# mLSTM's gates made in steps beside two scans, and 64x64 merge blocks whose directions take turns

## The chip, the cores and the metric

The kernel runs on one core of one Trainium2 chip. The number of a run is the device time of one execution, in microseconds. Three runs of the kernel before gave 1412.16, 1409.82 and 1408.49 us, so its time is a median of 1409.82 us.

A core has engines with a queue each, and each queue is worked off in order: PE (matrix products), DVE (elementwise work, scans along a row), ACT (functions and scaled copies), POOL (elementwise work), and SP, which here only issues DMA transfers. An instruction that waits for another engine or for a transfer holds up everything that is queued behind it on its own engine.

## The reference, cut to what matters

One layer: a norm, one projection into two mixers (gated DeltaNet, GDN, with 8 heads, and mLSTM with 4), each run over the tokens in both directions, then a merge, an output projection and a gated MLP. There are 256 context tokens and 512 latent tokens. What the change touches are mLSTM's gates and the triangular solve of GDN:

```
ig = soft_cap(ml_i + ml_igate_b)                 # soft_cap(x) = 15 * tanh(x / 15)
lf = log_sigmoid(soft_cap(ml_f + ml_fgate_b))
m_t = max(lf_t + m_{t-1}, ig_t)                  # the stabiliser, by direction and head
bc = cumsum(lf) in each chunk
dmat = bc[:, None] - bc[None, :] + ig[None, :]   # then exp(dmat - m_t): mLSTM's weights
...
# GDN, by head and direction:
a_strict = (k * beta) @ k^T * decay
sol = triangular_solve(a_strict, rhs, lower, unit_diagonal)
```

mLSTM's gates are needed when its first head is prepared and scanned, after all of GDN's scans but the last few. GDN's solve is done by an explicit inverse of blocks of 128 tokens, built from 16x16 inverses (POOL) by merges of 16, 32 and 64 (PE).

## The kernel before, in words

Weights are streamed from memory, split on ACT and POOL or DVE into a high and a low part (L102, L103), and multiplied in three passes (`mm3`, L113 and L114). Head h of GDN is prepared by `gdn_prep(h)`: projections k, q, v, z (`acc`, in two PSUM banks that take turns, so that a projection starts when the one before the last has been read out by `conv_silu`, L595 to L599, or by L724 and L726), the decay rows `Eg` (loaded by DMA from `gd`, the GDN gates' own transposed rows, L631; finished on DVE by L646 and on ACT by L647; two buffers), the products of k with itself (`pkk`, L701 and L704), the 16x16 inverses (`inverses`: DVE cuts the diagonal blocks out, L765 to L767, a DMA `scr` and one back, a chain on POOL, L778 and L780, DMAs `scx` and `cdx`, and back into SBUF on ACT by L805), the products of q and k (L709, L713).

`merges(h)` then makes the inverse of a 128 block: `y0p` and `w0p` from 16 to 32 rows (L812, L819), `y1p` and `wp` from 32 to 64 (L844, L852), `y2p` and `w2p` from 64 to 128 (L865, L873). Each product is a matmul on a part of the array, named by its row and column strips. Each of the two directions has its own order of blocks. `gdn_scan(h)` is the scan over six chunks, `gdn_tail` what follows it.

`gdn_gates` makes GDN's gates from the gates' logits `Z` (128 rows by 768 tokens, in `oTg`, which is free until the first head's result is written at its end). The rows for the decays go through a copy `grr` (L502) and a DMA to `gd` (L504), and the DMAs of `Eg` and `qs` read `gd`.

`ml_gates` (L506 to L586) makes mLSTM's gates from the same logits: a tanh of all of `Z` (L520), a log sigmoid (L524 to L527), two cumulative sums in two directions and the running maximum in two directions (the five scans L531 to L535), the differences from chunk to chunk (L540 to L567), three exponentials (L564, L568, L569), two DMAs out (`r1d`, `ged`), two back in (`ge`), and twelve transposes on PE (L582) with four copies (L583) into `colA` and `colB`.

What sets the order: the program is written as Python generators; `drive` (L1128) takes a scan's steps, and between them the steps of other work (`bulk`, the preparation of a head three further on, and `side`, such as the next head's merges at the steps in `MERGE`). The text's order gives each instruction a priority; a scheduler then lays each engine's queue, and takes an instruction of lower priority ahead where it holds its operands and the engine would be idle by the scheduler's own reckoning. A `follow` adds a tie: this instruction stays behind an anchor on its engine. Before, `ml_gates` is written between the preparation of heads 0 to 2 and the first merges, with a priority that is `LATER` = 400 places down (L1170 to L1173) and with its first instruction tied behind the last `conv_silu` on ACT.

Of the kernel before, what the change touches and what calls it, by code (L numbers as in the profile page):

```python
# [60 lines left out]
LATER = 400  # L61
# [7 lines left out]
class Kern:  # L69
# [355 lines left out]
    def gates_rows(self, psx, psc):  # L425
# [4 lines left out]
        Z = self.grow[0]  # L430
# [75 lines left out]
    def ml_gates(self):  # L506

        nc, cp, hold = self.nc, self.cp, self.hold
        Q = 64
# [16 lines left out]
        nc.scalar.activation(t2, t2, AF.Ln, bias=1.0)
        nc.vector.scalar_tensor_tensor(L, z, 0.0, t2, ALU.min, ALU.subtract)  # L527
# [3 lines left out]
        nc.vector.tensor_tensor_scan(G[F, :], rm[F, :], L[F, :], 0.0, ALU.mult, ALU.add)  # L531
# [43 lines left out]
        for d in range(2):  # L575
            nc.sync.dma_start(self.ge[:, d, 8:12].rearrange("p r c -> p (r c)"),
                              ged[32 * d + 8 : 32 * d + 12, :].rearrange("r c -> (r c)").unsqueeze(0).broadcast_to([P, 4 * NCH]))
        for (T_, col) in ((TA, self.colA), (TB, self.colB)):
            for (c0, c1) in ((0, 4), (4, 6)):
                ps = self.pt([P, 512], "prep", "ps_gt")  # L580
                for c in range(c0, c1):
                    nc.tensor.transpose(ps[:, (c - c0) * P : (c - c0 + 1) * P], T_[:, c * P : c * P + P], self.ident)  # L582
# [203 lines left out]
    def merges(self, h):  # L786
# [750 lines left out]
```

## Time and profile before

| | |
|---|---|
| median of three runs | 1409.82 us (1408.49 to 1412.16) |
| the profiled execution | 1413.52 us, of which the span from first to last instruction is 1411.6 us |
| PE busy | 1326.0 us (94%), mean granted clock 0.966 |
| DVE / ACT / POOL busy | 908.5 us / 588.5 us / 507.8 us |
| head 0's scan begins on PE (L919) | at 187.8 us |
| mLSTM's gates on DVE | from 141.9 to 182.4 us |
| merges of heads 0 to 7 | from 150.4 to 591 us |

A row of the timeline view gives start, length, engine, source line, operation, the tiles written and read, a count, and in brackets how long its engine had been idle before it and what ended that. A row of the windows view gives, for a stretch, its length, the busy time of each engine with the number of its instructions, the granted clock of PE (1.00 is full speed), the share of the DMA engines and GB/s.

### The profile page before, as it was taken

The numbers are of one execution on the slowest core, as the hardware profiler recorded it, in microseconds if no ns is written. First come the engines' busy times: TensorE is split into PE (matmuls) and PEld (weight loads), VectorE is DVE, ScalarE is ACT, GpSimd is POOL, SyncE is SP. The second block draws the span as 40 slices with busy tenths as digits, with TensorE's granted clock in tenths as the row PEclk, the third lists the DMA queues.
The fourth block names the chain that finished last, engine by engine and source line by source line (L and its number), as shares of the span: only waits on it lengthen the run. The fifth ranks groups of instructions, "written<-read, shape, count | busy, mean of one in ns | idle before, by whom it ended". The sixth has DMA issues, their size and how long they took to land. (4 is left out here: it accounts for less than half of the span.)

```text
span 1411.6 us, 24202 instructions
## 1 busy us (share of the span) xinstructions
PE 1326.0 (94%) x9436; PEld 1121.7 (79%) x9436; DVE 908.5 (64%) x1860; ACT 588.5 (42%) x1283; POOL 507.8 (36%) x626
## 2 busy tenths in 40 slices
PE   5888699999999999999899999999989999999997
PEld 4777588878887887889788877788878888888886
DVE  6748973748575774655654464644559879879933
ACT  6555554545555554323233334432234333333331
POOL 4426131130321303243735662000135555555552
PEclk9999799999999999999999999999989999999999
DMA  8633233231322322354524442364323333233321
GB/s 244 152 88 93 56 80 83 74 102 37 89 77 69 82 50 77 106 151 117 144 75 112 114 118 61 98 202 139 126 69 111 90 98 102 84 104 90 104 90 60
DMA packets 233232, 141.85 MB, mean 100 GB/s; under 512 B 32977, under 2 KB 215518, under 8 KB 233118
## 3 DMA queue, kind: packets, MB, share of 16 engines
q1 hardware_dynamic: 233118, 140.31, 35.3%
q8 instruction: 74, 1.21, 0.4%
q14 instruction: 40, 0.33, 0.1%
HBM read 134.47 MB, written 5.82 MB: 99 GB/s over the span
## 5 line engine op out<-in xcount | busy, mean ns | idle before, releaser
L1507 DVE SCALAR_TENSOR_TENSOR y<-pu,fw,y 128x441 f32<-128x441 f32 (+2 forms) x352 | 230.0, 691 | 38.5 <-ACT y L1498 32.9
L137 POOL TENSOR_TENSOR rs<-pw_t,mhalf 128x1 f32<-128x1 f32 x14 | 8.2, 584 | 168.3 <-DVE pw_t L136 168.3
L137 POOL TENSOR_TENSOR kh<-pw_t,phalf 128x6 f32<-128x6 f32 x8 | 11.1, 1390 | 124.1 <-DVE pw_t L136 124.1
L293 POOL TENSOR_TENSOR aw<-aw,sc 128x512 f32<-128x512 f32 x32 | 40.0, 1256 | 31.1 <-DMA aw<-in_w_ada_dram 31.0
L915 DVE SCALAR_TENSOR_TENSOR X<-p,colA,vt 128x128 f32<-128x128 f32 x80 | 24.3, 346 | 33.9 <-PE p L911 33.7
L797 POOL TENSOR_TENSOR qs<-qs,qT 128x512 f32<-128x512 f32 x16 | 20.8, 1304 | 62.2 <-DMA qs<-gd 50.1
L773 POOL MEMSET gx<- 96x16 f32 x8 | 1.0, 123 | 115.4 <-DMA gx<-scr 115.4
L927 ACT ACTIVATE v<-p,sc 128x128 f32<-128x128 f32 x80 | 25.4, 367 | 34.4 <-PE p L919 34.3
L931 PE MATMUL p<-v,kt 128*128 128x128 f32 x160 | 29.8, 302 | 10.5 <-ACT v L927 10.5
L778 POOL TENSOR_TENSOR iv_t<-gx 96x14 f32<-96x14 f32 (+6 forms) x112 | 36.0, 322 | 7.5
L1076 DVE SCALAR_TENSOR_TENSOR C<-C,ge,mpc 128x257 f32<-128x257 f32 x32 | 15.3, 479 | 36.3 <-PE mpc L1072 36.2
L780 POOL TENSOR_TENSOR gx<-gx,iv_t 96x14 f32<-96x14 f32 (+6 forms) x112 | 34.8, 311 | 8.6
L1498 ACT ACTIVATE y<-pu,fw 128x512 f32<-128x512 f32 x44 | 30.0, 683 | 16.1 <-PE pu L114 6.8
L931 PEld LDWEIGHTS p<-v,kt 128*128 128x128 f32 x160 | 23.0, 195 | 16.8 <-ACT v L927 14.9
L646 DVE SCALAR_TENSOR_TENSOR Eg<-Eg,colA,mask 128x128 f32<-128x128 f32 x96 | 33.1, 411 | 3.9 <-DMA Eg<-gd 3.9
L1449 POOL TENSOR_TENSOR al<-y,ah 128x512 fp32r<-128x512 f32 x22 | 28.7, 1304 | 17.3 <-ACT ah L1448 15.8
L1281 DVE SCALAR_TENSOR_TENSOR x<-x,py 128x512 f32<-128x512 f32 x16 | 11.0, 686 | 36.6 <-PE py L114 36.6
L938 DVE SCALAR_TENSOR_TENSOR S<-S,ge,p 128x128 f32<-128x128 f32 x64 | 19.3, 343 | 18.2 <-PE p L931 17.1
L911 PE MATMUL p<-S,kT 128*128 128x128 f32 x160 | 29.9, 289 | 0.0
L944 ACT ACTIVATE v<-p,sc 128x128 f32<-128x128 f32 x64 | 23.1, 378 | 15.8 <-PE p L931 15.0
L1459 DVE TENSOR_TENSOR fd_t<-pd,m 128x512 f32<-128x512 f32 x8 | 5.3, 685 | 37.5 <-PE pd L114 37.5
L598 ACT ACTIVATE cv_t<-cv_y 128x512 f32<-128x512 f32 (+1 forms) x40 | 21.8, 546 | 17.2 <-DVE cv_y L597 14.2
(1235 smaller groups left out, 4699.4 us busy)
## 6 DMA issues: line engine op xcount, KB each, us to landing
aw<-in_w_ada_dram SPq DMA_DIRECT2D x41, 256.0 KB
uw<-in_w_ada_dram SPq DMA_DIRECT2D x16, 512.0 KB
Eg<-gd SPq DMA_DIRECT2D x16, 384.0 KB
gx<-in_w_ada_dram SPq DMA_DIRECT2D x23, 256.0 KB
qs<-gd SPq DMA_DIRECT2D x16, 256.0 KB
xn<-in_x_dram SPq DMA_DIRECT2D x4, 512.0 KB
Em<-r1d SPq DMA_DIRECT2D x8, 256.0 KB
mwo_0r<-in_w_in_dram SPq DMA_DIRECT2D x4, 512.0 KB
```

The source lines that it names most:

```text
L293: eng.tensor_tensor(w, w, self.sc[:, 4 * i : 4 * i + 4, 0:1].broadcast_to([P, 4, P]), ALU.mult)
L646: self.follow(nc.vector.scalar_tensor_tensor(E[:, c, :], E[:, c, :], self.colA[:, c, d, row : row + 1], self.mask[d], ALU.add, ALU.min), "v")
L778: eng.tensor_tensor(t, Bi[:, 0:j, j : j + 1].broadcast_to([8 * NB, j, n]), Bi[:, j : j + 1, j + 1 :].broadcast_to([8 * NB, j, n]), ALU.mult)
L780: g = eng.tensor_tensor(Bi[:, 0:j, j + 1 :], Bi[:, 0:j, j + 1 :], t, ALU.add)
L911: g = nc.tensor.matmul(p1[:, d, :], kT[:, c * P : c * P + P], S[d], start=True, stop=True)
L915: self.anchor["v"] = nc.vector.scalar_tensor_tensor(X[d], p1[:, d, :], self.colA[:, c, 2 + d, h : h + 1], vt[:, c, :], ALU.mult, ALU.subtract)
L927: nc.scalar.activation(v3[d], p2[:, d, :], AF.Copy, scale=sc[d][:, 2 + j, c : c + 1])
L931: g = nc.tensor.matmul(p3[:, d, :], kt[:, c, :], v3[d], start=True, stop=True)
L944: nc.scalar.activation(v2, p2[:, d, :], AF.Copy, scale=sc[d][:, j, c : c + 1])
L1449: nc.gpsimd.tensor_tensor(al[:, j, :], ys[0], ah[:, j, :].bitcast(F32), ALU.subtract)
L1498: nc.scalar.activation(y, ps, AF.Copy, scale=tap(0, 0))
L1507: g = nc.vector.scalar_tensor_tensor(o, u3[:, r0 + dy : r1 + dy, c0 + dx : c1 + dx], tap(dy, dx), o, ALU.mult, ALU.add)
```

## The change

Two things. First, `ml_gates` becomes a generator: its body is cut by `yield` into steps, eight of which are handed out at the odd steps of head 0's scan (`MLG` = 8) and the others at the even steps of head 1's scan. It no longer borrows tiles `kt` and `vt` from the heads: all of its values live in the five rows of `oTg`, with `Z` now in the last row and with sums and scans written over rows that are no longer read. The tie of its first instruction and the `LATER` priority are gone, and its twelve transposes are tied behind PE's anchor. Second, in `y2p` and `w2p` the loop over the directions is now the inner one, so that successive products belong to different directions.

```diff
-LATER = 400
+MLG = 8
...
-        Z, t2, L, M, G = self.grow
-        t2, L, M, G = (x[:Q, :] for x in (t2, L, M, G))
-        TB = hold.tile([P, NALL], F32, tag="kt", name="gTB", bufs=3)
-        m = hold.tile([P, NALL], F32, tag="vt", name="gm", bufs=3)[:Q, :]
-        rm = TB[:Q, :]
+        R0, TB, R2, TA, Z = self.grow
+        t2, G, L, M, z = (x[:Q, :] for x in (R0, TB, R2, TA, Z))
+        rm, m = t2, z
...
-        self.follow(nc.scalar.activation(Z, Z, AF.Tanh, scale=1.0 / CAP), "a")
+        nc.scalar.activation(Z, Z, AF.Tanh, scale=1.0 / CAP)
+        yield
         nc.vector.tensor_scalar(Z, Z, CAP, None, ALU.mult)
         nc.scalar.copy(M, Z[Q:, :])
+        yield
...
         nc.vector.tensor_tensor_scan(G[F, :], rm[F, :], L[F, :], 0.0, ALU.mult, ALU.add)
+        yield
         nc.vector.tensor_tensor_scan(G[B, ::-1], rm[B, :], L[B, ::-1], 0.0, ALU.mult, ALU.add)
+        yield
...
-        nc.vector.tensor_tensor(TA[:Q, :], M, G, ALU.subtract)
+        yield
+        nc.vector.tensor_tensor(M, M, G, ALU.subtract)
+        yield
...
-        nc.vector.tensor_tensor(ch(t2), ch(r1), bc(tot), ALU.add)
-        nc.scalar.activation(TA[Q:, :], t2, AF.Exp)
+        nc.vector.tensor_tensor(ch(G), ch(r1), bc(tot), ALU.add)
+        nc.scalar.activation(TA[Q:, :], G, AF.Exp)
+        yield
...
-                    nc.tensor.transpose(ps[:, (c - c0) * P : (c - c0 + 1) * P], T_[:, c * P : c * P + P], self.ident)
+                    self.follow(nc.tensor.transpose(ps[:, (c - c0) * P : (c - c0 + 1) * P], T_[:, c * P : c * P + P], self.ident))
                 nc.vector.tensor_copy(col[:, c0:c1, :, 8:12], ...)
+                yield
...
-        for d, (B, Dm) in enumerate(DD):
-            a, b = hs[d]
-            for c in range(NCH):
+        for c in range(NCH):
+            for d, (B, Dm) in enumerate(DD):
+                a, b = hs[d]
                 g = nc.tensor.matmul(y2p[b, c, :], B[a, c, b], Dm[a, c, m64(a)], start=True, stop=True, tile_position=(a.start, b.start))
...
-        p = tc.cur_priority
-        tc.cur_priority = p + LATER
-        self.ml_gates()
-        tc.cur_priority = p
+        gates = self.ml_gates()
...
+            if s < 2:
+                side.append((islice(gates, MLG), range(1, 100, 2)) if s == 0 else (gates, range(0, 100, 2)))
```

What the scheduler makes of it, in the built program, at three places (the order names the running sums and maxima L531 to L535, L532 to L539 in the changed program, as SCALAR_TENSOR_TENSOR; the trace calls them TENSOR_TENSOR_SCAN). Line numbers of the changed program are 12 to 13 higher in the part after `ml_gates` (L610 is the old L597, L612 the old L599, L659 the old L646, L739 the old L726, L819 the old L806, L818 the old L805, L940 the old L927, L1262 the old L1250).

DVE while head 0 is prepared, around `grr`, from which the decay rows of all heads are loaded. Before:

```order
L482 COPY gr<-ps_gs 128x6x8
L596 SCALAR_TENSOR_TENSOR cv_y<-pc_v_1184,cw,cv_y 128x255
L597 SCALAR_TENSOR_TENSOR cv_y<-px_q_1012,cw,cv_y 128x511
L482 COPY gr<-ps_gs 128x6x8
L493 COPY colA<-gr 128x6x8
L597 SCALAR_TENSOR_TENSOR cv_y<-pc_v_1184,cw,cv_y 128x255
L599 SCALAR_TENSOR_TENSOR qT_1011<-cv_t,cv_y 128x512
L491 TENSOR_SCALAR colA<-ps_gs 128x2x6x8
L493 COPY colA<-gr 128x6x8
L599 SCALAR_TENSOR_TENSOR vT_1177<-cv_t,cv_y 128x256
L502 COPY grr<-ps_gr 96x256
```

Now, from the same first row to the copies behind the scans, and then the piece around `grr`:

```order
L482 COPY gr<-ps_gs 128x6x8
L527 SCALAR_TENSOR_TENSOR oTg<-oTg 64x768
L610 SCALAR_TENSOR_TENSOR cv_y<-px_q_1012,cw,cv_y 128x511
L609 SCALAR_TENSOR_TENSOR cv_y<-pc_v_1184,cw,cv_y 128x255
L482 COPY gr<-ps_gs 128x6x8
L493 COPY colA<-gr 128x6x8
L536 SCALAR_TENSOR_TENSOR oTg<-oTg 32x768
L538 SCALAR_TENSOR_TENSOR oTg<-oTg 32x256
L532 SCALAR_TENSOR_TENSOR oTg<-oTg 32x768
L534 SCALAR_TENSOR_TENSOR oTg<-oTg 32x768
L610 SCALAR_TENSOR_TENSOR cv_y<-pc_v_1184,cw,cv_y 128x255
L612 SCALAR_TENSOR_TENSOR qT_1011<-cv_t,cv_y 128x512
```

```order
L548 TENSOR_TENSOR oTg<-oTg,s_2839 32x6x64 x2
L555 COPY s_2839<-s_2839 32x1
L556 COPY s_2839<-s_2839 32x1
L557 COPY s_2839<-s_2839 32x3
L576 TENSOR_TENSOR s_2839<-s_2839 64x6
L502 COPY grr<-ps_gr 96x256
L564 TENSOR_TENSOR oTg<-oTg 64x768
L568 TENSOR_TENSOR oTg<-oTg 64x768
L571 TENSOR_TENSOR s_2839<-s_2839 64x6
L609 SCALAR_TENSOR_TENSOR cv_y<-px_v_1216,cw,cv_y 128x511
```

So the steps that are written beside the scans of heads 0 and 1 stand, on DVE, ahead of `grr` and right behind it: the logits and the rows are there, and the scheduler takes the steps where it reckons DVE idle. L527, L532 to L539 and L545 to L577 of the changed program are all in this place; only the last copies into `colA` and `colB` stand at the end of head 1's scan.

DVE while head 1 is finished and head 2 begun, around `zs` of head 1 (its bank of PSUM is the next projection's) and around L806, which the first merge waits for. Before:

```order
L726 SCALAR_TENSOR_TENSOR zs_1673<-z_t,px_z_1646 128x512
L103 TENSOR_TENSOR wq2l<-wq2r,wq2h 128x1024
L524 SCALAR_TENSOR_TENSOR oTg<-oTg 64x768
L806 STREAM_TRANSPOSE gx<-gx 128x384
L713 TENSOR_TENSOR at_0_1571<-pqk_1566,Eg_0_1346 128x512
L713 TENSOR_TENSOR at_1_1573<-pqk_1566,Eg_1_1348 128x512
L596 SCALAR_TENSOR_TENSOR cv_y<-pc_k_1780,cw,cv_y 128x255
L527 SCALAR_TENSOR_TENSOR oTg<-oTg 64x768
L597 SCALAR_TENSOR_TENSOR cv_y<-pc_k_1780,cw,cv_y 128x255
L531 SCALAR_TENSOR_TENSOR oTg<-gTB,oTg 32x768
L532 SCALAR_TENSOR_TENSOR oTg<-gTB,oTg 32x768
L533 SCALAR_TENSOR_TENSOR gm<-oTg 32x768
```

Now:

```order
L726 TENSOR_TENSOR at_0_1571<-pqk_1566,Eg_0_1346 128x512
L726 TENSOR_TENSOR at_1_1573<-pqk_1566,Eg_1_1348 128x512
L612 SCALAR_TENSOR_TENSOR vT_1575<-cv_t,cv_y 128x512
L103 TENSOR_TENSOR wq2l<-wq2r,wq2h 128x1024
L659 SCALAR_TENSOR_TENSOR Eg_0_1744<-Eg_0_1744,colA,mask_89 128x128 x6
L739 SCALAR_TENSOR_TENSOR zs_1673<-z_t,px_z_1646 128x512
L819 STREAM_TRANSPOSE gx<-gx 128x384
L659 SCALAR_TENSOR_TENSOR Eg_1_1746<-Eg_1_1746,colA,mask_94 128x128 x6
L609 SCALAR_TENSOR_TENSOR cv_y<-pc_k_1712,cw,cv_y 128x255
```

The gates' instructions have left this stretch. The products `at` (the old L713) have come ahead of `zs`, and so has the finishing of head 2's first decay rows, `Eg_0`, which waits for a DMA.

ACT where head 1's scan ends and head 2's begins. Before:

```order
L102 CAST wq4h<-wq4r 128x1024
L739 ACTIVATE junk,ssq_3641<-ps_tm_q_3636 128x128
L1250 ACTIVATE ge_5_3651<-px_g_5_3658 128x512
L805 ACTIVATE gx<-cdx_3324,pm 128x12x16 x2
L739 ACTIVATE junk,ssq_3641<-ps_tm_q_3636 128x128
L927 ACTIVATE v_2_3702<-p_2_3699,sc_0_2154 128x128
```

Now:

```order
L752 ACTIVATE junk,ssq_3625<-ps_tm_q_3620 128x128 x3
L818 ACTIVATE gx<-cdx_3288,pm 128x12x16 x2
L752 ACTIVATE junk,ssq_3625<-ps_tm_q_3620 128x128
L102 CAST wq4h<-wq4r 128x1024
L1262 ACTIVATE ge_5_3635<-px_g_5_3642 128x512
L940 ACTIVATE v_2_3700<-p_2_3697,sc_0_2086 128x128
```

The split of a weight and the read-out of a projection have gone behind the two instructions that wait for `cdx`, and so ahead of the scan's first scaled copy.

More of the change, by code (lines that the diff above doesn't have):

```diff
@@ L429, in gates_rows @@
         self.grow = [rows[:, NALL * i : NALL * (i + 1)] for i in range(5)]
-        Z = self.grow[0]
+        Z = self.grow[4]
         nc.scalar.activation(Z[:, :NCTX], psc[:, :NCTX], AF.Identity, bias=self.gb)
@@ L454, in gdn_gates @@
         nc, cp, hold = self.nc, self.cp, self.hold
-        Z = self.grow[0]
+        Z = self.grow[4]
         z = hold.tile([P, 4, NCH, GH], F32, tag="at0", name="gz", bufs=3)
@@ L543, in ml_gates @@
             nc.vector.tensor_tensor(Gc[s, :, a], Gc[s, :, a], tot[s, :].unsqueeze(2).broadcast_to([32, NCH, 64]), ALU.subtract)
+        yield
         for (s, e) in ((F, 127), (B, 0)):
@@ L551, in ml_gates @@
         nc.vector.tensor_copy(min_[B, CC : NCH - 1], mend[B, CC + 1 :])
+        yield
         def bc(x):
             return x.unsqueeze(2).broadcast_to([Q, NCH, P])
-        r1, TA = L, Z
+        r1 = L
         nc.vector.tensor_tensor(r1, G, m, ALU.subtract)
@@ L559, in ml_gates @@
         nc.sync.dma_start(self.r1d, r1)
-        nc.vector.tensor_tensor(TA[:Q, :], M, G, ALU.subtract)
+        yield
+        nc.vector.tensor_tensor(M, M, G, ALU.subtract)
+        yield
         nc.vector.tensor_tensor(tot, tot, min_, ALU.add)
-        nc.vector.tensor_tensor(ch(t2), ch(r1), bc(tot), ALU.add)
-        nc.scalar.activation(TA[Q:, :], t2, AF.Exp)
+        nc.vector.tensor_tensor(ch(G), ch(r1), bc(tot), ALU.add)
+        nc.scalar.activation(TA[Q:, :], G, AF.Exp)
+        yield
         nc.vector.tensor_tensor(last, last, mend, ALU.subtract)
-        nc.vector.tensor_tensor(ch(t2), ch(TA[:Q, :]), bc(last), ALU.add)
-        nc.scalar.activation(TB[:Q, :], t2, AF.Exp)
+        nc.vector.tensor_tensor(ch(L), ch(M), bc(last), ALU.add)
+        nc.scalar.activation(TB[:Q, :], L, AF.Exp)
         nc.scalar.activation(TB[Q:, :], m, AF.Exp, scale=-1.0)
+        yield
         s6b = cp.tile([P, NCH], F32, tag="s6b", name="s6b")[Q:, :]
@@ L577, in ml_gates @@
                               ged[32 * d + 8 : 32 * d + 12, :].rearrange("r c -> (r c)").unsqueeze(0).broadcast_to([P, 4 * NCH]))
+        yield
         for (T_, col) in ((TA, self.colA), (TB, self.colB)):
@@ L581, in ml_gates @@
                 for c in range(c0, c1):
-                    nc.tensor.transpose(ps[:, (c - c0) * P : (c - c0 + 1) * P], T_[:, c * P : c * P + P], self.ident)
+                    self.follow(nc.tensor.transpose(ps[:, (c - c0) * P : (c - c0 + 1) * P], T_[:, c * P : c * P + P], self.ident))
                 nc.vector.tensor_copy(col[:, c0:c1, :, 8:12], ps[:, : (c1 - c0) * P].rearrange("p (c q t) -> p c q t", q=4, t=32)[:, :, :, 8:12])
+                yield
         self.dump("colA", self.colA)
@@ L869, in merges @@
         w2p = self.pt([P, NCH, 64], "mg", f"w2p{h}")
-        for d, (B, Dm) in enumerate(DD):
-            a, b = hs[d]
-            for c in range(NCH):
+        for c in range(NCH):
+            for d, (B, Dm) in enumerate(DD):
+                a, b = hs[d]
                 g = nc.tensor.matmul(w2p[a, c, :], y2[b, c, :], B[b, c, b], start=True, stop=True, tile_position=(b.start, a.start))
```

3 lines of the change are left out of this document (1 added, 2 removed).

## The prediction

> **What bounds the kernel now.** I read the page's first two parts, then PE's busy time by windows, and where PE stood idle the timelines of PE and of what released it.
>
> ```profile
> span 1411.6 us, 24202 instructions
> PE 1326.0 (94%) x9436; PEld 1121.7 (79%) x9436; DVE 908.5 (64%) x1860; ACT 588.5 (42%) x1283; POOL 507.8 (36%) x626
> ```
>
> PE sets the end: a change gains where it shortens PE's queue or takes idle time out of it. Windows of 5 us (PE, PEld, DVE, ACT, POOL, clock, DMA) show the largest hole:
>
> ```profile
> 150.00:155.00 5.00, 3.07 (x108) 2.18 (x106) 4.33 (x4) 4.92 (x16) 0.00 (x0) 0.99 0.45 140
> 155.00:160.00 5.00, 0.00 (x0) 0.00 (x0) 4.94 (x13) 1.50 (x5) 0.00 (x0) 0.50 0.00 0
> 160.00:165.00 5.00, 1.13 (x85) 1.17 (x89) 4.90 (x15) 1.29 (x2) 0.00 (x0) 0.50 0.00 0
> 170.00:175.00 5.00, 2.51 (x51) 2.17 (x52) 4.72 (x12) 4.62 (x11) 2.42 (x8) 0.70 0.25 59
> ```
>
> DVE is full there and PE empty, at half its clock. PE's timeline says for what, DVE's what stood ahead of it:
>
> ```profile
> 163.87 1.48 PE L819 MATMUL w0p<-gx,y 32*32 32x16 f32 x96 [10.80 <-DVE y L814]
> 171.52 0.22 PE L844 MATMUL y1p<-Dm,gx 32*32 32x32 f32 x2 [1.70 <-DVE Dm L824]
> 178.08 1.13 PE L852 MATMUL wp<-gx,y 32*32 32x32 f32 x48
> ...
> 151.91 1.74 DVE L531 TENSOR_TENSOR_SCAN oTg<-gTB,oTg 32x768 f32<-32x768 f32 x1
> 163.16 0.55 DVE L814 COPY y<-y0p 128x384 f32<-128x384 f32 x1
> 169.88 0.34 DVE L821 TENSOR_TENSOR gx<-gx,w0p 128x192 f32<-128x192 f32 x1
> 176.39 0.36 DVE L846 COPY y<-y1p 128x192 f32<-128x192 f32 x1
> ```
>
> L814 stands behind mLSTM's scans. The windows of DVE's instructions on the gates' rows `oTg`, ahead of L814 and behind it:
>
> ```profile
> 140.00:163.10 23.10, 8.65 (x9) 0.82 0.29 77
> 163.10:178.00 14.90, 6.68 (x11) 0.61 0.27 60
> ```
>
> **Part 1: the gates leave the hole.** In the built order they don't go beside the scans of heads 0 and 1. DVE takes them at about 82 to 112 us, around `grr`. So the sum is over one stretch, from there to `wp`, which DVE's queue paces before. What happens early:
>
> ```profile
> 96.13 0.42 DVE L502 COPY grr<-ps_gr 96x256 f32<-96x256 f32 x1 [5.46 <-PE ps_gr L500]
> 98.36 0.82 SPq L631 DMA_DIRECT2D Eg<-gd  x2
> 102.23 1.67 DVE L646 SCALAR_TENSOR_TENSOR Eg<-Eg,colA,mask 128x128 f32<-128x128 f32 x6 [2.38 <-DMA Eg<-gd]
> 107.01 2.42 DVE L646 SCALAR_TENSOR_TENSOR Eg<-Eg,colA,mask 128x128 f32<-128x128 f32 x1
> 110.15 0.67 DVE L726 SCALAR_TENSOR_TENSOR zs<-z_t,px_z 128x512 f32<-128x512 f32 x1
> ...
> 97.77 2.41 POOL L103 TENSOR_TENSOR wk1l<-wk1r,wk1h 128x1024 fp32r<-128x1024 f32 x1 [14.51 <-ACT wk1h L102]
> 106.91 2.38 POOL L103 TENSOR_TENSOR wq1l<-wq1r,wq1h 128x1024 fp32r<-128x1024 f32 x1
> ...
> 110.88 1.22 PE L113 MATMUL px_k<-hx,wk1h 128*128 128x512 f32 x2 [3.73 <-DVE zs L726]
> ```
>
> Before, DVE was idle for 5.46 us ahead of `grr`: it had come free at 90.67. Now it has ahead of it L521, L524, L527, the five scans, both L543 and the small copies: of the 15.33 us in the two windows all but L557, L560, L563 and L567, which are some 0.95 each (3.8), and with about 0.8 of copies between small tiles: 12.3 us. `grr` starts at 90.67 + 12.3 + about 0.5 (waits for the Ln on ACT) = 103.5, which is **+7.4**. The decay rows follow it through two DMAs (102.23 less 96.55, 5.7 us), and with them `zs`, for whose bank PE waits: the idle 3.73 us become some 6. Two more things push: `r1d` now stands on SP ahead of the loads of `Eg`, and it waits for L557; and L557 falls on POOL's split of wk1, which can no longer start at 97.77: its high part waits on ACT behind the exp of the maximum (L569), so for about 102.8. How two such instructions meet stands above: a row of L646 takes 2.42 us in place of its 0.33 while POOL's split runs from 106.91 to 109.29. I take +1.0 for this, and +0.3 for L571 and L572 and their waits. So px_k starts at **+8.7**, at about 119.6.
>
> The Trainium skill (SBUF — State Buffer, Who interferes with whom) has a rule for this: a DVE instruction with two SBUF inputs and a POOL instruction that reads SBUF exclude each other for a whole instruction. The trace agrees, with the 2.42 us above. By the rule each of the moved scans may also lose up to a split's 2.4 us; by the rows POOL is idle from 83.3 until wk1's high part, so that only the pieces around `grr` are met, and the sum keeps its 1.0.
>
> From px_k to L814, DVE loses what it had there: 8.65 us, and the 1.18 us it waited for the Ln (the row follows): **-9.8**. Against that, `Eg` of head 2 now stands ahead of `zs` and L806. Its DMA can start only when L713 has freed the buffer, then takes 3.87 us (98.36 to 102.23), and only a copy and a split, 0.6 and 1.2 us, stand between: **+2.2**.
>
> ```profile
> 150.64 0.95 DVE L527 SCALAR_TENSOR_TENSOR oTg<-oTg 64x768 f32<-64x768 f32 x1 [1.18 <-ACT oTg L526]
> 176.67 1.48 PE L582 MATMUL ps_gt<-ident,oTg 128*128 128x128 f32 x6
> 176.78 0.75 DVE L596 SCALAR_TENSOR_TENSOR cv_y<-px_k,cw,cv_y 128x511 f32<-128x511 f32 x1
> ```
>
> L814 ends at +1.1. Behind it: w0p ended at 165.35 and L821 began at 169.88, behind gates (-4.5); L563, 0.95, stood in L824's way, and L567 with two copies, 1.4, in that of L846: **-6.9**. The two L596/L597 of px_k now come ahead of L846, 0.75 each: **+1.5**. `wp` stood on PE behind six transposes which are no longer there, from 176.75 to 178.08: **-1.3**. Sum: 8.7 - 9.8 + 2.2 - 6.9 + 1.5 - 1.3 = **-5.6 us** at `wp`, and PE is nearly full behind it, so it lasts. Bounds: if all of the early work lay in idle time, PE would get back the 10.80, the 1.70 and about 5.5 of half clock from 163.87 to 178.08, **-18**; if the whole +8.7 stayed and nothing behind L814 were gained, **+9.6** (8.7 + 2.2 - 1.3).
>
> **Part 2: the border of heads 1 and 2.** PE waits there for the first scaled copy of the scan, and that for a DMA:
>
> ```profile
> 313.10 0.79 PE L931 MATMUL p<-v,kt 128*128 128x128 f32 x2 [3.30 <-ACT v L927]
> ...
> 306.62 1.05 ACT L102 CAST wq4h<-wq4r 128x1024 fp32r<-128x1024 f32 x1 [3.01 <-PE px_g L113]
> 307.83 0.59 ACT L1250 ACTIVATE ge<-px_g 128x512 f32<-128x512 f32 x1
> 311.74 0.80 ACT L805 ACTIVATE gx<-cdx,pm 128x192 f32<-128x192 f32 x2 [3.32 <-DMA cdx<-scx]
> 312.69 0.61 ACT L927 ACTIVATE v<-p,sc 128x128 f32<-128x128 f32 x2
> ...
> 288.08 0.37 SPq L768 DMA_DIRECT2D scr<-cdx  x1
> ```
>
> In the new order the cast and L1250 stand behind L805 and ahead of L927: 1.05 + 0.59 = **+1.6**. What hid them, the 3.32 us of waiting, is then gone for them. The twelve transposes (about 0.82 us for six at full clock, by half of the 1.48 above) now lie here, eight of them ahead of L931: the idle time covers them, at nothing; uncovered they cost 1.6 more. The four copies, 0.2 each, lie in DVE's idle time.
>
> **Part 3: the directions take turns.** The rows of three kinds of product, at full clock:
>
> ```profile
> 261.34 0.69 PE L819 MATMUL w0p<-gx,y 32*32 32x16 f32 x60
> 268.11 0.59 PE L844 MATMUL y1p<-Dm,gx 32*32 32x32 f32 x30
> 290.57 1.43 PE L873 MATMUL w2p<-gx,y 64*64 64x64 f32 x24
> L844 PE MATMUL y1p<-Dm,gx x240: 184/191/257, 171.5 to 509.5; 32*32 32x32 f32 x120
> L873 PE MATMUL w2p<-gx,y x120: 218/218/267, 185.0 to 529.2; 64*64 64x64 f32 x120
> ```
>
> Less one matmul's own length (0.191 and 0.218 us), y1p's 29 steps take 13.8 ns each, w2p's 23 steps 52.7. In y1p the strips alternate between two row groups; in w2p one direction, one row group, comes twelve pieces in a row. A 64-wide piece has twice the columns, so it would take 2 x 13.8 = 27.6 with alternating strips. Half of 52.7 times 23 gives **0.6 us a group**, for 16 groups (eight heads, y2p and w2p). Bounds: 0, and 9.7 for all. Not all of it reaches the end. Between `scr` and `cdx` lies a fixed chain of DMAs and POOL (288.08 to 311.74), and at five borders like the one above PE waits for it:
>
> ```profile
> PE p L931 <- ACT v L927: 10.5, 6, 3.3
> ```
>
> w2p of heads 2 to 6 starts some 2 us behind its `scr` (290.57 against 288.08): there PE would only wait longer. Eleven groups are left: 11 x 0.6 = **-6.6**.
>
> The Trainium skill has a rule against it (TensorEngine Tiling (Array Packing), Gotcha 1: PSUM Pressure): different row tiles cannot use one PSUM bank at the same time, and both directions write one bank. By it the term is 0. The row of y1p, which also has two row groups and one bank, speaks for overlap.
>
> **Sum.** -5.6 + 1.6 - 6.6 = -10.6. The profiled execution, 1413.52 us (its span of 1411.6 and 1.9 around it), would become 1402.9. It was 3.7 above the median; from the median of 1409.82 I get **1399.2 us**.
>
> **Rivals.** (a) *The directions still run one after the other*, by the rule above: -5.6 + 1.6, **1405.8**. For it: no row has 64-wide pieces of two row groups side by side. Against: y1p's 13.8 ns. (b) *The early steps hide in idle time*: then the hole goes whole, -18 + 1.6 - 6.6, **1387**. For it: DVE is idle 5.46 and 2.38 us there. Against: `grr` stands behind 12.3 us of gates in the order. (c) *Slower: the late `grr` is passed on whole.* The place is the loads of `Eg`: if from px_k on the queue is paced by the three round trips of `Eg` and not by DVE's work, the work taken off DVE returns nothing: +9.6 + 1.6 - 6.6, **1414.4**. It decides from where L814 ends some 10 us later than before, past 173. For it: each round trip is 5.7 us and two of them now wait behind L713. Against: from 155 to 165 DVE was busy 4.9 of 5. (d) *The borders take back part 3 too*, also the y2p of heads 2 to 6 (3.0) and what heads 0, 1 and 7 gain: -5.6 + 1.6, **1405.8** as in (a), but with short y2p rows.
>
> **Chances.** Forecast 0.47, with a range of its own of 1393 to 1405; (a) 0.17; (b) 0.13; (c) 0.12; (d) 0.11. A measurement of this kernel tells about 0.3% (4.2 us) from no change, so faster means under 1405.6. The forecast and (b) give 0.60, and (a) and (d), which lie on the edge, about a third of their 0.28: faster 0.68. Their rest gives same 0.20; (c) slower 0.12. The range: 1388 to 1412.
>
> **What would show it.** Right: `grr` on DVE at 103 to 104, px_k near 119.6 with some 6 us idle; L814 within 3 us of 163.16, the idle time ahead of w0p under 2 us; `wp` near 172.5; at the border after head 1's scan the idle 3.3 us grow to near 5; 24 pieces of w2p in about 0.8 us; idle time at the borders of heads 2 to 6 longer by 0.6 each. Wrong: w2p still at 1.43 (a); px_k before 114 (b); L814 past 173 (c); y2p at 0.8 and the gaps at the borders longer by 1.2 (d).

## The result, and the profile after

The changed kernel took 1423.73 us (median of six runs, 1422.83 to 1425.60), the kernel before 1409.86 us (six runs, 1405.60 to 1412.16). The ratio is 1.0104 with a 95% interval of 1.0087 to 1.0120: it is **slower, by about 14 us**. The prediction was 1399.2 us, and its range ended at 1412. The profiled execution after took 1422.89 us with a span of 1421.1.

What the prediction said of the start is read from the timeline of DVE in the changed kernel (start, duration, engine, line, operation, and in brackets the idle time ahead of it with what ended it). The line numbers are those of the changed kernel, 12 or 13 higher than before behind the gates and some less within them: L827 is the old L814, L659 the old L646.

```profile
104.16 2.21 DVE L557 COPY s<-s 32x3 f32<-32x3 f32 x1
...
106.48 0.41 DVE L502 COPY grr<-ps_gr 96x256 f32<-96x256 f32 x1
...
113.25 1.67 DVE L659 SCALAR_TENSOR_TENSOR Eg<-Eg,colA,mask 128x128 f32<-128x128 f32 x6 [1.50 <-DMA Eg<-gd]
114.95 0.16 DVE L582 COPY s6b<-oTg 32x6 f32<-32x6 f32 x1
115.12 1.21 DVE L583 COPY s6b<-oTg 32x6 f32<-32x6 f32 x1
116.36 1.71 DVE L612 SCALAR_TENSOR_TENSOR vT<-cv_t,cv_y 128x512 f32<-128x512 f32 x1
117.99 3.73 DVE L659 SCALAR_TENSOR_TENSOR Eg<-Eg,colA,mask 128x128 f32<-128x128 f32 x6
121.65 0.68 DVE L739 SCALAR_TENSOR_TENSOR zs<-z_t,px_z 128x512 f32<-128x512 f32 x1
...
139.88 1.75 DVE L659 SCALAR_TENSOR_TENSOR Eg<-Eg,colA,mask 128x128 f32<-128x128 f32 x6 [4.07 <-DMA Eg<-gd]
...
153.69 2.16 DVE L717 SCALAR_TENSOR_TENSOR Bt<-pkk,sc,Eg 128x128 f32<-128x128 f32 x8 [2.48 <-PE pkk L714]
...
164.23 1.66 DVE L659 SCALAR_TENSOR_TENSOR Eg<-Eg,colA,mask 128x128 f32<-128x128 f32 x6 [1.78 <-DMA Eg<-gd]
...
172.84 1.52 DVE L778 STREAM_TRANSPOSE cg<-Bt 32x192 f32<-32x192 f32 x4 [2.50 <-PE y0p L825]
174.38 0.56 DVE L827 COPY y<-y0p 128x384 f32<-128x384 f32 x1
```

`grr` came at 106.48 (before 96.13; predicted 103 to 104) and L827 at 174.38 (before 163.16; predicted within 3 us of that). Between `px_k` and L827 DVE no longer has gates to do, but its four longest waits there, for transfers and for PE, make 10.8 us. The timeline of PE in the changed kernel:

```profile
122.38 1.22 PE L113 MATMUL px_k<-hx,wk1h 128*128 128x512 f32 x2 [7.42 <-DVE zs L739]
...
175.09 0.98 PE L832 MATMUL w0p<-gx,y 32*32 32x16 f32 x96 [1.39 <-DVE y L827]
...
188.51 0.92 PE L886 MATMUL w2p<-gx,y 64*64 64x64 f32 x24
...
199.83 0.80 PE L944 MATMUL p<-v,kt 128*128 128x128 f32 x2 [6.01 <-ACT v L940]
```

The hole ahead of `w0p` has shrunk from 10.80 to 1.39 us, but PE itself arrives there 21 us later (it began the product before it, `y0p`, at 150.43, and now begins it at 171.77): it waits 7.42 us ahead of `px_k` in place of 3.73, and again behind it. And there is a new wait of 6.01 us at the first product with v (0.79 before). What ends it stands in two queues of the changed kernel, first that of the DMAs (SP), then that of ACT:

```profile
175.77 0.37 SPq L781 DMA_DIRECT2D scr<-cdx  x1
...
192.13 0.33 SPq L795 DMA_DIRECT2D scx<-gx  x1
193.83 0.36 SPq L796 DMA_DIRECT2D cdx<-scx  x1
```

```profile
196.69 0.80 ACT L818 ACTIVATE gx<-cdx,pm 128x192 f32<-128x192 f32 x2 [6.58 <-DMA cdx<-scx]
...
199.43 0.61 ACT L940 ACTIVATE v<-p,sc 128x128 f32<-128x128 f32 x2
```

The scaled copy v (L940) stands on ACT behind L818, which waits for the inverse blocks of head 1. Their chain (`scr`, POOL, `scx`, `cdx`) starts at 175.77; before, it started at 167.48. So PE at the first product of **head 0** waits for work of **head 1** that it does not need.

To see where the rest went, the windows view was taken in slices of 2 us, and in each the time that PE was not busy (idle) and its busy time by 1 less the granted clock (lost to half clock) were summed. The stretches end at the first piece of `w2p` of head 0 and at the first projection of mLSTM behind GDN's last scan (the row that waits for `mwk1l`). All in us:

| | before | after |
|---|---|---|
| to `w2p` of head 0 | 185.0: idle 41.2, half clock 14.1 | 188.5: idle 43.6, half clock 14.8 |
| from there to mLSTM's first projection | 433.2: idle 15.6, half clock 8.1, work 409.5 | 441.4: idle 27.4, half clock 9.5, work 404.5 |
| the rest, to PE's last products | 784.3: idle 21.2, half clock 14.1 | 782.2: idle 24.0, half clock 8.8 |

Only 3.5 us of the loss are there at `w2p` of head 0. Another 8.1 come in the scans of GDN, where the work became 5 us less and the idle time 11.8 us more. By the starts of `w2p` the loss is all there after the first scan: the changed kernel is 12.4 us behind at head 1 (240.66 against 228.30) and 11.3 at head 7. The last row's difference looks like chance: the other runs below have 6 to 13 us of half clock there, and the profiled execution of before has 14.1. That one lay 3.7 us above its median, and the two profiles differ by only 9.4 us.

### The profile page after: what moved, and what is told of

It is laid out like the page before. It is cut to its first block, busy times and chain, and to the rows that moved or that the text cites. A ratio compares the mean times of both kernels' runs of the same rounds, so it can differ in the third digit from the quotient of the medians.

```text
span 1421.1 us, 24204 instructions
## 1 busy us (share of the span) xinstructions
PE 1319.0 (93%) x9436; PEld 1112.6 (78%) x9436; DVE 911.0 (64%) x1860; ACT 587.5 (41%) x1283; POOL 509.9 (36%) x626
## 3 DMA queue, kind: packets, MB, share of 16 engines
q8 instruction: 74, 1.21, 0.4%
## 5 line engine op out<-in xcount | busy, mean ns | idle before, releaser
L793 POOL TENSOR_TENSOR gx<-gx,iv_t 96x14 f32<-96x14 f32 (+6 forms) x112 | 37.4, 334 | 8.7
L940 ACT ACTIVATE v<-p,sc 128x128 f32<-128x128 f32 x80 | 25.4, 367 | 35.6 <-PE p L932 35.5
L659 DVE SCALAR_TENSOR_TENSOR Eg<-Eg,colA,mask 128x128 f32<-128x128 f32 x96 | 31.3, 394 | 7.4 <-DMA Eg<-gd 7.4
```

The costliest lines, as they stand in the source:

```text
L659: self.follow(nc.vector.scalar_tensor_tensor(E[:, c, :], E[:, c, :], self.colA[:, c, d, row : row + 1], self.mask[d], ALU.add, ALU.min), "v")
L793: g = eng.tensor_tensor(Bi[:, 0:j, j + 1 :], Bi[:, 0:j, j + 1 :], t, ALU.add)
L940: nc.scalar.activation(v3[d], p2[:, d, :], AF.Copy, scale=sc[d][:, 2 + j, c : c + 1])
```

## The experiments

Each run was timed 4 to 12 times, beside the kernel before on the same chip. "Ratio" is to that kernel, with its 95% interval. The runs come from three chips, so runs of different groups are best compared by their ratios.

| run | edit | median, us | ratio |
|---|---|---|---|
| turns_only | before, with the turns | 1407.98 | 1.0003 (0.9982 to 1.0023) |
| gates_only | the change, without the turns | 1418.73 | 1.0071 (1.0047 to 1.0095) |
| gates_held | the change, gates tied to the scans | 1407.40 | 0.9995 (0.9974 to 1.0017) |
| grr_first | the change, gates behind `grr` | 1422.53 | 1.0100 (1.0074 to 1.0127) |
| border_only | before, new order at the borders | 1388.92 | 0.9843 (0.9804 to 0.9882) |
| border_turns | the same with the turns | 1387.45 | 0.9841 (0.9810 to 0.9873) |
| border_held | with turns and held gates | 1379.82 | 0.9788 (0.9756 to 0.9819) |
| border_after | the change, new order at the borders | 1399.67 | 0.9911 (0.9876 to 0.9947) |
| border_pow | border_only, and the power ahead of `qs` | 1380.96 | 0.9805 (0.9783 to 0.9828) |
| border_pow_turns | the same with the turns | 1375.89 | 0.9778 (0.9750 to 0.9805) |
| border_pow_after | the change, with both orders | 1381.71 | 0.9799 (0.9771 to 0.9826) |
| border_pow_held | turns, held gates, both orders | 1366.23 | 0.9707 (0.9684 to 0.9730) |

### The two halves of the change apart

**The turns alone** are the second half of the diff put into the kernel before, in y2p and likewise in w2p:

```
-        for d, (B, Dm) in enumerate(DD):
-            a, b = hs[d]
-            for c in range(NCH):
+        for c in range(NCH):
+            for d, (B, Dm) in enumerate(DD):
+                a, b = hs[d]
```

> The kernel before with nothing but the turn-taking of the directions in y2p and w2p; the gates are left as they were. In the changed kernel a group of 24 pieces took 0.92 us in place of 1.43, so 16 groups are 8.2 us less work for PE. Theory A (the chain scr to cdx paces the borders of the heads, so PE waits longer by what it saves): the groups take 0.92 us, the idle time of PE ahead of L931 and L897 from 300 to 620 us grows from 13 us by 4 to 7, and the time is 1406 to 1411. Theory B (the gain of the prediction, 11 groups of 0.51 us): 1404 or less, with the idle time at the borders up by less than 3 us. Theory C (the turns themselves cost, by longer chains on POOL at heads 5 and 7): 1413 or more, and the 14 steps on POOL take 15 us instead of 13.8 there.

Measured: 1407.98 us, no change; theory A. The groups took 0.92 us, so 16 groups are 8.2 us less work. PE's waits from 290 to 575 us, the waits view with its columns "engine, line waited for: us in total, times, longest us", first of the kernel before, then of this run:

```profile
PE p L931 <- ACT v L927: 9.7, 5, 3.3
PE po L897 <- ACT o L964: 2.7, 2, 1.6
```

```profile
PE p L931 <- ACT v L927: 12.5, 5, 4.9
PE po L897 <- ACT o L964: 4.2, 2, 2.2
```

The starts of the waits' ends show the gain being given back, border by border: 313.10, 377.29, 431.23, 494.11 and 549.46 before; 311.30, 374.29, 429.27, 493.14 and 549.21 here. Three us ahead at the second border, 0.25 at the fifth. By the account in slices the stretch from `w2p` of head 0 to mLSTM's first projection has 7.2 us less work, 4.8 us more idle time and 2.6 us more half clock. Theory C has a grain of truth: the chain from `gx<-scr` to `cdx<-scx` of head 5 took 16.7 us here and 15.5 before.

**The gates alone** are the changed kernel with the old loops in y2p and w2p (the diff above, reversed).

> The changed kernel with the old order in y2p and w2p: the gates of the mLSTM in steps, the directions one after the other. Theory A (the gates carry the whole loss, by grr 10 us late; the turns are nearly neutral): 1421 to 1427, grr at 106 and px_k at 122 as in the changed kernel, PE idle 5 to 7 us ahead of the first product with v of head 0. Theory B (the turns gain 5.6 and so hide part of the loss): 1428 to 1432. Theory C (the turns carry part of the loss): 1413 to 1419.

Measured: 1418.73 us, ratio 1.0071. `grr` stood at 106.38 and `px_k` at 121.93, and the waits view from 180 to 215 us has the wait for v:

```profile
PE p L944 <- ACT v L940: 4.5, 1, 4.5
```

It is theory A's mechanism, with a time just inside C's range (1413 to 1419) and a wait below A's 5 to 7 us. The gates carry most of the loss, 10 of the 14 us by the ratios. Whether the turns add the rest is not settled: the intervals of this ratio and of the whole change's (1.0087 to 1.0120) overlap.

### The place of the gates

**Gates held to the scans.** The scheduler had moved the steps, written beside scans 0 and 1, up into idle time of DVE ahead of `grr`. This run ties the tanh behind the last conv on ACT and the first DVE instruction of each step behind the running scan's last DVE instruction:

```
-        nc.scalar.activation(Z, Z, AF.Tanh, scale=1.0 / CAP)
+        self.follow(nc.scalar.activation(Z, Z, AF.Tanh, scale=1.0 / CAP), "a")
-        nc.vector.tensor_scalar(Z, Z, CAP, None, ALU.mult)
+        self.follow(nc.vector.tensor_scalar(Z, Z, CAP, None, ALU.mult), "v")
...      (likewise the first DVE instruction of each later step, up to L571)
```

> The changed kernel with its gates truly held to the scans: the Tanh is ordered behind the last conv on ACT, and the first DVE instruction of each step behind the last DVE instruction of the running scan. In the built order grr stands again ahead of all gates, w0p of head 0 has none ahead of it, and the steps lie between the scans' updates of heads 0 and 1. Theory A (the place of the gates was the fault, and the work itself is cheap): px_k starts at 110 to 112, the idle time ahead of w0p is under 2 us where before had 10.8, and the time is 1388 to 1398, faster than both. Theory B (DVE's scans, 1.75 us each, get into the way of the updates X and S, on which PE waits): the hole is gone but PE waits 10 to 18 us more for L928 and L951 in heads 0 and 1, and the time is 1402 to 1412. Theory C (the start is paced by the DMA trips and by the chain scr to cdx anyway): L827 of head 0 not earlier than 160, 1408 or more.

Measured: 1407.40 us, the time of the kernel before (1407.36 on that chip), so the place of the gates is worth the change's whole loss. Of theory A the start is right: `px_k` at 111.39, L827 at 158.64, `w2p` of head 0 at 173.99, 11 us ahead of before. Its waits from 100 to 230 us:

```profile
PE p L944 <- ACT v L940: 6.8, 2, 4.9
PE w0p L832 <- DVE y L827: 5.2, 1, 5.2
```

Half of the hole ahead of `w0p` stays with no gate in its way, since L827 stands on DVE behind L659, which waits for the DMA of `Eg`:

```profile
153.95 3.24 DVE L659 SCALAR_TENSOR_TENSOR Eg<-Eg,colA,mask 128x128 f32<-128x128 f32 x12 [3.10 <-DMA Eg<-gd]
...
158.64 0.56 DVE L827 COPY y<-y0p 128x384 f32<-128x384 f32 x1
```

The lead of 11 us was gone at `w2p` of head 1 (230.20, before 228.30): from `w2p` of head 0 to there PE had 8.4 us of idle time and 4.7 of half clock, where before had 0.9 and none. Theory B's price came, but not from its cause: its waits for the updates X and S are not among those above; the waits are for v, behind the DMA `cdx`.

**Gates behind `grr`.** One edge more in the changed kernel:

```
-        nc.vector.tensor_scalar(Z, Z, CAP, None, ALU.mult)
+        self.queue_after(nc.vector.tensor_scalar(Z, Z, CAP, None, ALU.mult), self.anchor_grr)
```

(`anchor_grr` is the copy L502.)

> The changed kernel with one edge more: the first DVE instruction of the gates is ordered behind the copy grr. The same gates then lie on DVE from about 98 to 135 us, among the work of heads 0 and 1. Theory A (the delay of grr and of the two round trips behind it was the loss): grr at 95 to 97, px_k at 111 to 114, and the time is 1405 to 1414. Theory B (it is the 18 us of DVE work ahead of L827 that costs, wherever they stand): px_k early, but L827 of head 0 again at 172 to 176, the first product with v of head 0 again waits 5 to 7 us, and the time is 1420 to 1426.

Measured: 1422.53 us; theory B. `grr` at 97.83 and `px_k` at 113.32 were nearly where they had been before, and L827 still came at 172.22. From 100 to 230 us:

```profile
PE pkk L714 <- ACT kt L684: 7.5, 2, 7.3
PE w0p L832 <- DVE y L827: 6.1, 1, 6.1
PE px_k L113 <- DVE zs L739: 4.5, 1, 4.5
```

So it was not `grr` as such. B's wait for v has another name here: PE waits 7.3 us ahead of `pkk` for `kt` (L684), and that copy stands on ACT behind the same L818, which waits 6.71 us for `cdx`. L827 came at 158.64 with no gates ahead of it on DVE, at 163.16 with the 8.65 us of before, and at 172.22 and 174.38 with all of them, behind or ahead of `grr`. The four times go with how much of the gates is done before head 0's merges. The gates' instructions on ACT and POOL and their transfers moved together with those on DVE, and no run parts them, so DVE's share alone is not shown.

### The borders

In all runs so far, and in before, the copy of `cdx` (L805, L818) stands on ACT ahead of the running scan's scaled copies v. The next run ties it behind them, and writes the next head's merges two steps later, so that `y0p` moves behind 15 projections. L805 belongs to the first of these merge steps, so the later steps alone also move it down in the text; no run has only one of the two edits:

```
-MERGE = (1, 2, 4, 6, 8, 10, 11)
+MERGE = (3, 4, 5, 7, 8, 10, 11)
-                    nc.scalar.activation(v3[d], p2[:, d, :], ...)
+                    self.anchor["s"] = nc.scalar.activation(v3[d], p2[:, d, :], ...)
-            nc.scalar.activation(U[:, :, 16 * i : 16 * i + 16], cx, ...)
+            self.follow(nc.scalar.activation(U[:, :, 16 * i : 16 * i + 16], cx, ...), "s")
```

> The kernel before with one idea alone, neither turns nor gates changed: the ACT copy that waits for cdx (L805) is ordered behind the running scan's scaled copies v, and the merges of the next head are written two steps later (3, 4, 5, 7, 8, 10, 11 in place of 1, 2, 4, 6, 8, 10, 11). In the built order L805 then follows v of the scan's second stage, and y0p stands 15 projection matmuls (3.5 us) behind that stage's product with v. Theory A (PE's idle time at the borders is only ACT's queue: v stands behind a copy that waits for a DMA): the waits for L927 and L964 from 300 to 620 us, 12.7 us in before, fall under 4, the half clock behind them goes too, and the time is 1388 to 1398. Theory B (the chain from scr to cdx sets the pace of a head, wherever its end is waited for): the idle time moves to y0p and to the later merges, and the time is 1404 to 1412.

Measured: 1388.92 us, ratio 0.9843; theory A. The waits of this run from 290 to 575 us, and its ACT at the second border:

```profile
PE p L931 <- ACT v L927: 2.2, 4, 0.6
PE po L897 <- ACT o L964: 1.1, 2, 0.9
```

```profile
314.34 1.15 ACT L964 ACTIVATE o<-po,fo 128x128 f32<-128x128 f32 x4 [3.48 <-POOL fo L961]
...
316.09 0.64 ACT L927 ACTIVATE v<-p,sc 128x128 f32<-128x128 f32 x2
316.59 0.83 ACT L805 ACTIVATE gx<-cdx,pm 128x192 f32<-128x192 f32 x2
```

L805 no longer waits, since `cdx` has landed, and v no longer waits for it. The two edits together were worth 21 us, more than all that the change had aimed at; how much the tie alone is worth is not shown.

**With the turns** on top of it:

> The same, and the directions take turns in y2p and w2p. Theory A (the borders absorbed what the turns saved; with the borders free the 8.2 us reach the end): 5 to 9 us below the run with the border order alone. Theory B (the turns save nothing that counts): within 3 us of it.

Measured: 1387.45 us: no gain that can be told. PE now waits 8.4 us for o (L964), in five places of which the longest is 3.1 us. That copy waits for the power `fo` on POOL, and on POOL of this run one sees why:

```profile
310.23 1.41 POOL L797 TENSOR_TENSOR qs<-qs,qT 128x512 f32<-128x512 f32 x1 [6.75 <-DMA qs<-gd]
311.60 1.01 POOL L961 TENSOR_TENSOR fo<-fo,mhalf 128x4 f32<-128x4 f32 x1
```

The power, whose input was ready at 305.86 (L960 on DVE starts at 305.69 and takes 0.17), stands behind a product that waits for a DMA. It is the same fault on another queue. Theory B was right on the time, and its other wait has a name.

**The held gates and the hoisted gates, with the border order.** In both the edits stand together as shown above.

> The border order, the turns and the held gates together. Theory A (the lead of 7 us that the held gates had at the first product with v of head 0 was lost at the borders): 4 to 8 us below the run with border order and turns. Theory B (it was lost to DVE's gates among the updates of scans 0 and 1): within 3 us of it, or above.

> The changed kernel, gates hoisted ahead of grr as they are, with the border order. Theory A (of the loss of 14 us, some 8 came from the first wait for v of head 0, 6.0 us and its half clock, and the rest from the late grr): that wait is under 1 us, and the time is 8 to 12 us above the run with border order and turns. Theory B (the late grr passes on whole, wherever it is waited for): 14 us or more above it.

Measured: 1379.82 us for the held gates, 7.6 us below border_turns, as theory A said, though the intervals of the two ratios overlap. 1399.67 us for the hoisted ones, 12.2 us above border_turns: at A's edge, and not where A had it. At `w2p` of heads 0, 1 and 2 that run is 3.1 us behind border_turns; the rest comes after 516 us, with more waits for o.

### The second wait

POOL's products `qs` are tied behind the power of the head before:

```
-        nc.gpsimd.tensor_tensor(f, f, self.mhalf[:, 0:XC], ALU.pow)
+        self.anchor["q"] = nc.gpsimd.tensor_tensor(f, f, self.mhalf[:, 0:XC], ALU.pow)
-            nc.gpsimd.tensor_tensor(x, x, qT, ALU.mult)
+            self.follow(nc.gpsimd.tensor_tensor(x, x, qT, ALU.mult), "q")
```

> The kernel before with the border order (L805 behind v of the scan's second stage, merges two steps later) and one edit more: POOL's product qs (L797), which waits for a DMA, is ordered behind the power fo (L961) of the head before; no turns. In the run with the border order alone PE's idle time from 290 to 600 us is already only 6 us. Theory A (nothing more to be had without the turns): within 3 us of that run, 1386 to 1392. Theory B (the power sets the pace all the same): 5 us or more below it.

> The same with the turns in y2p and w2p. With the border order and the turns PE waited 2.9, 3.1 and 1.2 us for o (L964), which waited for the power fo on POOL, which stood behind qs and its DMA: a second wait that took over what the turns saved. Theory A (that wait is what hid the turns' 8.2 us): the waits for L964 fall under 1 us each and the time is 4 to 9 us below the run without turns. Theory B (the turns are not worth their 8 us, or another wait takes it again): within 3 us of it.

> The same with the turns and the held gates. Theory A (the gates' place is worth its 7 us at the first product with v, and nothing takes it back): 5 to 9 us below the run with turns, 1370 to 1378. Theory B: within 3 us of it.

> The changed kernel, gates hoisted ahead of grr as they are, with the border order and the power ahead of qs. With the border order alone it stood 3.1 us behind the run without the hoisted gates (border order and turns) at w2p of heads 0, 1 and 2, but 12 us behind at the end, with more waits for o (L977) on the way. Theory A (the late grr itself costs 3 us, and the rest of the loss of 14 us arises at the borders): 1376 to 1382, a ratio to before of 0.978 to 0.982. Theory B (the late start costs 10 us or more, also where the borders are free): 1385 to 1390, a ratio of 0.984 to 0.988.

Measured: 1380.96 without turns, 8.0 us below border_only by the medians and 5 by the ratios, whose intervals overlap: theory B by the medians, not clear of the noise. With turns, 1375.89, the power's new place is clear of it: the interval (0.9750 to 0.9805) lies below that of border_turns (0.9810 to 0.9873), some 9 us by the ratios. Between the two new runs, the turns gain 5.1 us by the medians, as theory A said, and 4 by the ratios, whose intervals overlap. The profiles agree with a gain: from `w2p` of head 0 to mLSTM's first projection border_pow takes 407.6 us (186.16 to 593.73) and border_pow_turns 400.2 (184.68 to 584.91), in one profile each. The waits of border_pow_turns from 290 to 575 us:

```profile
PE p L931 <- ACT v L927: 1.0, 2, 0.6
PE po L897 <- ACT o L964: 0.8, 1, 0.8
```

So most of the turns' 8.2 us now reaches the end of GDN's scans, and before it had gone to these two waits; at the kernel's end the gain is 4 to 5 us, not clear of the noise. With the held gates 1366.23 us, 9.7 us below border_pow_turns and clear of the noise: theory A, with a little more than its 5 to 9 us. With the hoisted gates of the change 1381.71, theory A as well: 3.3 us behind border_pow_turns at `w2p` of head 0 (187.96 against 184.68) and 5.0 behind at mLSTM's first projection. Free of the border waits, the hoisted gates cost some 3 us by the ratios and 6 by the medians in place of 14, and the two intervals overlap.

**border_pow_held is the version that beats both kernels**: 1366.23 us, 0.9707 of before (0.9684 to 0.9730). From `w2p` of head 0 to mLSTM's first projection it has 7.1 us of idle time and 1.7 of half clock, where before had 15.6 and 8.1. At its start one wait is left that none of these edits touches:

```profile
158.03 1.48 PE L832 MATMUL w0p<-gx,y 32*32 32x16 f32 x96 [4.92 <-DVE y L827]
```

## Why the prediction was wrong, step by step

- **"`grr` starts at 103.5, +7.4":** right in kind, too small. It came at 106.48, +10.4. Part of the difference is L557 (the old L551), a copy of 32x3 that took 2.21 us (others of that kind 0.13 to 0.16) while POOL's split of wk1 ran (2.60 us from 103.75).
- **"px_k starts at +8.7":** measured +11.5 (122.38 against 110.88). The 2.8 us too little lie ahead of `grr`; behind it 1.1 us were lost, and the prediction had 1.3. The term of +1.0 for meetings of DVE and POOL was mis-sized, by L557. POOL of the changed kernel, in the same stretch:

```profile
103.75 2.60 POOL L103 TENSOR_TENSOR wk1l<-wk1r,wk1h 128x1024 fp32r<-128x1024 f32 x1 [11.05 <-ACT wk1h L102]
115.03 2.48 POOL L810 TENSOR_TENSOR qs<-qs,qT 128x512 f32<-128x512 f32 x2 [8.69 <-DVE Eg L659]
117.48 2.79 POOL L103 TENSOR_TENSOR wq1l<-wq1r,wq1h 128x1024 fp32r<-128x1024 f32 x1
```

  Beside the last two, L659 took 3.73 us for six pieces (1.67 just before), L583, a copy like L582, 1.21 where L582 took 0.16, and L612 1.71, where its row of the same shape takes 0.68 at 159.68: 4.1 us too long, and with L557 6.2. But the kernel before had 4.1 us of this in the same place, in its second group of six pieces (1.67 just before):

```profile
104.42 5.81 DVE L646 SCALAR_TENSOR_TENSOR Eg<-Eg,colA,mask 128x128 f32<-128x128 f32 x6
```

  So some 2.1 us are new, for which the prediction had 1.0. The section of the Trainium skill that it quoted (SBUF — State Buffer, Who interferes with whom) also says that a copy on DVE can take the ports that POOL shares, and then the two block each other for a whole instruction. The trace agrees: two of the four are copies, which the prediction had counted at their plain price.
- **"From px_k to L814, -9.8":** this step failed: it took DVE's queue for the limit of the whole stretch, and PE's own time in it for given. The stretch took 52.0 us (122.38 to 174.38) where before took 52.3 (110.88 to 163.16). `y0p` is what L814, now L827, copies; its row of the kernel before, and then PE's waits and its row of the changed kernel:

```profile
150.43 0.38 PE L812 MATMUL y0p<-gx,cg 32*32 32x32 f32 x20
```

```profile
143.44 1.11 PE L636 MATMUL ps_tm_k<-ident,kT 128*128 128x128 f32 x4 [3.19 <-ACT kt L684]
...
166.54 1.07 PE L113 MATMUL px_k<-hx,wk2h 128*128 128x512 f32 x2 [2.29 <-DVE zs L739]
...
171.77 1.02 PE L825 MATMUL y0p<-gx,cg 32*32 32x32 f32 x96
```

  From the start of `y0p` to the copy, 12.7 us became 2.6: what left DVE was gained there. But from `px_k` to `y0p` PE took 49.4 us in place of 39.6. Its work, at full clock, was the same (37.4 and 37.3 us); 4.7 us more were idle time and 5.0 us more half clock, behind the 7.42 us ahead of `px_k` and behind these two waits. Both waits lead back to a transfer of `Eg`: zs stands on DVE behind L659, which waited for it until 164.23, and kt stands on ACT behind L660, which waited for the L659 of 139.88:

```profile
141.66 0.84 ACT L660 ACTIVATE Eg<-Eg 128x768 f32<-128x768 f32 x1 [2.30 <-DVE Eg L659]
```

  This is rival (c), priced with 0.12 and deciding "past 173": its round trips do set the pace, but by way of PE's waits and its clock, which (c) did not have. gates_held shows the other side: with all 8.65 us gone and `grr` on time, `y0p` came at 150.75, and L827 only 4.5 us earlier than before, behind the next transfer of `Eg`. (From its rows, the +2.2 for `Eg` in this part of the sum comes to 2.1.)
- **"-6.9, +1.5 and -1.3" behind L814:** right. `wp` was 5.0 us late where L827 was 11.2 late, so 6.2 were won back there.
- **"PE is nearly full behind it, so it lasts":** this sentence failed too, and no rival replaced it. At `wp` and at `w2p` the loss was only 5.0 and 3.5 us. But `scr` of head 1 was 8.3 us late, and through ACT's queue the first product with v came at 199.83 instead of 190.97, 8.9 us late. The rows for it (`scr`, `cdx`, L805 ahead of L927) stood in the prediction, for another border.
- **"The border of heads 1 and 2, +1.6":** the two instructions did move between L818 and L940, as predicted, and cost nothing: PE's idle time there was 2.26 us, less than the 3.30 before, since transposes and `y0p` stood ahead of the product.
- **"Half of 52.7 ns, 0.6 us a group":** right in kind; 0.92 us instead of 1.43 is 0.51. In the trace's single records the pieces of `w2p` of one direction start 58 ns apart in the kernel before; in turns they still do, and each starts 6 to 7 ns behind a piece of the other direction. So the two directions do overlap although both write one PSUM bank. The measurement decides against the rule that the prediction quoted from the Trainium skill (TensorEngine Tiling (Array Packing), Gotcha 1: PSUM Pressure), at least for two tiles that write different partitions, and rival (a) falls.
- **"Eleven groups are left: -6.6":** wrong; turns_only kept nothing of all sixteen. This is rival (d), whose 0.11 was too low. The error is the count: I took away only the groups that start behind `scr`. In turns_only a lead from any group was spent at the next borders, one or two heads later.
- **Left out of the sum:** what a wait costs beyond itself. Rival (c) gave 1414.4; the measured time is higher by 9.3, of which 6.6 are part 3's gain that did not come. The new waits' half clock stands in no term at all: 5.0 us ahead of `y0p`, and 2.2 behind the wait for v. That (c) lies nearest to the measured time is partly luck, since its +9.6 at `wp` was 5.0 and the wait for v of head 0 was not in it.

## What to carry to other kernels

Before work is moved or made shorter, look for the queue in which an instruction that the critical engine needs stands behind one that waits for a DMA: here, freeing one such place on ACT, with the next head's merges two steps later, was worth 21 us and one on POOL 5 to 9 more, while a saving of 8 us on the busiest engine showed no gain in time until they were gone. Steps that are written beside a loop need not run there: a scheduler that finds an engine free earlier will put them there, so tie them to the loop if the place matters. And if the same wait stands at every border of a loop, what is gained between borders is not yet won: follow it through the next borders before it goes into a sum.

## What the runs showed of the hardware

A wait of PE costs more than its length. In the changed kernel, behind the wait of 6.01 us (windows of 2 us; the fields behind POOL are the granted clock, the DMA share and GB/s):

```profile
196.00:198.00 2.00, 0.00 (x0) 0.00 (x0) 0.48 (x1) 1.27 (x5) 0.00 (x0) 0.86 0.92 259
198.00:200.00 2.00, 0.17 (x1) 0.17 (x2) 0.10 (x1) 1.91 (x11) 0.00 (x0) 0.50 0.00 0
200.00:202.00 2.00, 2.00 (x28) 1.71 (x29) 1.16 (x5) 0.84 (x4) 0.23 (x1) 0.50 0.04 8
202.00:204.00 2.00, 2.00 (x12) 2.00 (x10) 2.00 (x15) 0.00 (x0) 1.09 (x1) 0.50 0.00 0
204.00:206.00 2.00, 2.00 (x81) 1.57 (x81) 2.00 (x9) 0.51 (x2) 0.00 (x0) 0.93 0.00 0
```

PE works at half clock until 204, and by such slices it lost 2.2 us more. Over the 14 profiles of this study, counting waits behind 100 us that stand alone (no other of 0.9 us or more within 9 us), the loss came in steps of about 1.7 us, up to 3.4 (behind the longest waits also between the steps):

| wait, us | number | no loss | about 1.7 us | about 3.1 us |
|---|---|---|---|---|
| 0.9 to 1.9 | 56 | 40 | 14 | 2 |
| 1.9 to 2.6 | 41 | 14 | 25 | 2 |
| 2.6 to 4.0 | 47 | 2 | 31 | 14 |
| 4.0 to 8.0 | 20 | 0 | 8 | 12 |

So a wait of 3 us costs nearly 5 in all, and which waits cost extra is partly chance. This may be part of why runs of one kernel differ by some us: of the twelve of turns_only, the fastest, 1402.12 us, had a mean granted clock of 0.976 and the slowest, 1417.75 us, one of 0.961. The Trainium skill (TensorE: Matmul & The Clock Gate, Part 1: The HAM clock gate) says that the clock is set by the activity in windows of about 3.4 us that run freely. The trace agrees: in all 14 profiles each stretch of half clock, but for the last of a profile, lasts a whole number of 3.41 us, and the steps of 1.7 us are half of that. The advice of the Trainium skill on the same page (TensorE: Matmul & The Clock Gate, Why this matters for your kernels) to avoid gaps of more than about 3 us is too mild for this kernel: of 41 waits between 1.9 and 2.6 us, 27 were followed by a loss.
